# Loading the modulation's weights in blocks of 512 columns and writing four one-column products in a row

## The chip, the core and the metric

The kernel runs on one core of a Trainium2 chip. The time is the device time of one execution in microseconds (us), the median of the runs given. In the profile the engines are PE (TensorE's products) and PEld (its weight loads), DVE (VectorE), ACT (ScalarE), POOL (GpSimd) and SP (SyncE, which here only issues DMAs; SPq is its queue).

## What is computed

One decoder layer on a sequence of 1024 rows of 1024 values. The change touches one product of it, the first line here: the conditioning vector `c`, through SiLU, times a matrix of 1024 x 6144. The six parts of 1024 values shift, scale and gate the layer's two halves.

```
mod = silu(c) @ w_ada[l] + b_ada[l]
sh1, sc1, g1, sh2, sc2, g2 = [m[:, None, :] for m in jnp.split(mod, N_ADA, axis=-1)]
h = rmsnorm(x, norm1_gain[l]) * (1.0 + sc1) + sh1
proj = h @ w_in[l]
...   # stick-breaking, sliding-window and forgetting attention, a diagonal SSM, each on its columns of proj
x = x + g1 * (mixed @ w_out[l])
h = rmsnorm(x, norm2_gain[l]) * (1.0 + sc2) + sh2
x = x + g2 * (jnp.square(jax.nn.relu(h @ w_mlp_in[l])) @ w_mlp_out[l])
return rmsnorm(x, final_gain)
```

## The kernel before

The parts sh1 and sc1 are wanted at once and are made in `shift_scale` (its products are L217). The other four (indices 2 to 5: g1, sh2, sc2, g2) are made by the generator `ada_rest`, and that is what changes. It is called twice, for the parts (2, 4) and (3, 5). A call has one PSUM bank `ps` of 128 x 512: rows 0, 32, 64 and 96 each take one half (512 columns) of one of the two parts. For each of 8 slices `k` of the contraction and each of the two parts it loads the slice's 128 x 1024 weights (L303, 512 KB, tile `wa`, tag `U`, two buffers) and makes two products (L307). Each has a stationary operand of one column (`cact[:, k:k+1]`), 512 moving columns, and its own output row, so its own group of 32 columns of TensorE's array. After the eighth slice DVE adds the bias (`row`, L311) and SP stores the parts (L312).

The generator's steps are handed out by `beside(ada, 3)`, three to each of the 16 units of stick-breaking attention in `by_pair`. A unit is two `sb_row`: scores `z` (L639, with the mask's product L653), softmax on ACT and DVE, and in `mix` transposes `tp` (L700) and products with the values `pv` (L705). The products with the input weights follow in the program (`fm_unit`, `tm_unit`: L253, L254, L255 in `mm3`, three to a slice), and then the SSM (`ssm_main`: L857, L884, L886, L906), whose tiles share the tags `U` and `s4` with `ada_rest`.

What stands where on an engine is not the program's order: the tile framework's scheduler reorders all instructions by its own estimate of the times when it builds the kernel (`schedule_with_timeline_sim=True`), within the dependences. Engines and SP's queue then work strictly in the built order. Products of different kinds are so mixed on PE: attention, projections and the modulation stand between each other. Below, a visit is a run of modulation products (L307) between products of other kinds; a place where the kind changes is a change.

Of the kernel before, what the change touches and what calls it, by code (L numbers as in the profile page):

```python
# [9 lines left out]
F32 = mybir.dt.float32  # L10
# [9 lines left out]
P = 128  # L20
S = 1024
D = 1024
KT = D // P
# [10 lines left out]
def tile_trunk(ctx: ExitStack, tc: tile.TileContext, a: dict, out: bass.AP):  # L34
    nc = tc.nc
    V, A, G, T, SY = nc.vector, nc.scalar, nc.gpsimd, nc.tensor, nc.sync
# [6 lines left out]
    QD = [dram.tile([P, 3, S], F32, name=f"qd{i}") for i in range(6)]  # L43
    KD = [dram.tile([P, 2, S], F32, name=f"kd{i}") for i in range(5)]
# [28 lines left out]
    cact = const.tile([P, KT], F32, name="cact")  # L73
# [35 lines left out]
    NZ, TP, S4, NW, NWT = 2, 2, 8, 4, 2  # L109
# [80 lines left out]
    def turn(pst, tag, xs, f):  # L190
        ps = pst.tile([P, 4, P], F32, tag=tag, bufs=NZ if tag == "z" else 2, name="ps")
        for t in range(4):
            T.transpose(ps[:, t, :], xs[t][:, f * P:(f + 1) * P], ident)
        return ps.rearrange("p t k -> p (t k)")
# [95 lines left out]
                extra(t, ps)  # L290

    SPARE = lambda b: (ps1 if b else psm).tile([P, 512], F32, tag="tp" if b else "ss", bufs=TP if b else 1, name="ps")
    def ada_rest(js, wide, tile, row):

        ps = psm.tile([P, 512], F32, tag="ss", name="ps")
        for r in range(4):
            c0 = js[r // 2] * D + r % 2 * 512
            SY.dma_start(out=row[32 * r:32 * r + 1, :], in_=a["b_ada"][:, c0:c0 + 512])
        for k in range(KT):
            for i, j in enumerate(js):  # L300
                for c in range(0, D, wide):
                    w = tile()
                    SY.dma_start(out=w, in_=a["w_ada"][0, k * P:(k + 1) * P, j * D + c:j * D + c + wide])  # L303
                    yield
                    for n in range(wide // 512):
                        r = 2 * i + c // 512 + n
                        T.matmul(ps[32 * r:32 * r + 1, :], cact[:, k:k + 1], w[:, n * 512:(n + 1) * 512],  # L307
                                 start=k == 0, stop=k == KT - 1)
        for r in range(4):
            o = row[32 * r:32 * r + 1, :]  # L310
            V.tensor_tensor(o, ps[32 * r:32 * r + 1, :], o, op=ALU.add)  # L311
            SY.dma_start(out=MD[js[r // 2]][:, r % 2 * 512:r % 2 * 512 + 512], in_=o)  # L312

    def rest(x):
        for _ in x:
            pass

    v_sb = keep.tile([P, NT, 256], F32, name="v_sb")
# [273 lines left out]
    ssm = tc.alloc_tile_pool(name="ssm", bufs=1)  # L592
# [3 lines left out]
    def load_k(kd):  # L596

        kk = [[None, None], [None, None]]
        for n in (1, 0):
            for x in range(2):  # L600
                kk[x][n] = hd.tile([P, 512], F32R, tag="kk", bufs=KB, name="kk")
                SY.dma_start(out=kk[x][n].bitcast(F32), in_=kd[x * HD:x * HD + HD, :, n * 512:n * 512 + 512])
        return kk

    def load_q(qd, h, c0, c1):

        s = []
        for r in range(2):
            s.append(att.tile([P, c1 - c0], F32R, tag=f"s{r}", bufs=QB, name=f"s{r}"))
            load = SY.dma_start(out=s[r].bitcast(F32), in_=qd[h * HD:h * HD + HD, r:r + 2, c0:c1])  # L610
        return s, load.ins

    def by_pair(row, qd, kd, v, beside):

        nonlocal mark
        for p in range(2):
            kk = load_k(kd[p])
            for j in (3, 2, 1, 0):
                q = [load_q(qd[p], x, j * 256, j * 256 + 256) for x in range(2)]
                if (p, j) == MARK:  # L620
                    mark = q[1][1]
                cols_of = [slice(p * P + x * HD, p * P + x * HD + HD) for x in range(2)]
                pv, r = None, None
                for i in (2 * j, 2 * j + 1):
                    beside(8 * p + 6 - 2 * j + i % 2)
                    ws = []
                    for x in range(2):
                        w, r = row(q[x][0], kk[x], i, r, 2 * p + x)
                        ws.append([(w[:, b * P:(b + 1) * P], b) for b in range(i + 1)])
                    pv = mix(ws, v, cols_of, i, pv, r is not None)  # L630
                put(v[:, 2 * j:2 * j + 2, p * P:p * P + P], pv, r)
# [60 lines left out]
    def mix(ws, v, hs, i, pv, both):  # L692

        pv = pv or ps1.tile([P, 2, P], F32, tag="pv", bufs=1, name="pv")
        todo = [(x, ws[x][n], n) for n in range(len(ws[0])) for x in range(2)]
        for c in range(0, len(todo), 4):
            part = todo[c:c + 4]
            tp = ps1.tile([P, 4, P], F32, tag="tp", bufs=TP, name="tp")
            for b, (x, (w, kb), n) in enumerate(part):
                T.transpose(tp[:, b, :], w, ident)  # L700
            wt = att.tile([P, 4, P], F32, tag="wt", bufs=NWT, name="wt")
            copies[0] += 1
            (A.copy if copies[0] % 2 and both else V.tensor_copy)(wt[:, 0:len(part)], tp[:, 0:len(part)])  # L703
            for b, (x, (w, kb), n) in enumerate(part):
                T.matmul(pv[x * HD:x * HD + HD, i % 2, :], v[:, kb, hs[x]], wt[:, b, :],  # L705
                         start=n == 0, stop=n == len(ws[0]) - 1)
        return pv

    def put(o, pv, r):

        if r is None:
            V.tensor_copy(o, pv)
            return
        rw = att.tile([P, 2, 2, HD], F32, tag="rw", bufs=2, name="rw")
        V.tensor_copy(rw, r[:, :, :, None].to_broadcast([P, 2, 2, HD]))
        ps = ps1.tile([P, 2, P], F32, tag="tp", bufs=TP, name="ps")
        for t in range(2):
            T.matmul(ps[:, t, :], rw[:, t].rearrange("p x d -> p (x d)"), ident, start=True, stop=True)
        rb = att.tile([P, 2, P], F32, tag="rw", bufs=2, name="rb")
        A.copy(rb, ps)  # L720
        V.tensor_tensor(o, pv, rb, op=ALU.mult)
# [194 lines left out]
    def beside(x, n):  # L916
        def f(u):
            for _ in range(n):
                next(x, None)
        return f  # L920

    def ada_all():
        for js in ((2, 4), (3, 5)):
            yield from ada_rest(js, D, lambda: ssm.tile([P, D], F32, tag="U", bufs=2, name="wa"),
                                ssm.tile([P, 512], F32, tag="s4", bufs=S4, name="row"))

    ada = ada_all()
    by_pair(sb_row, QD[0:2], KD[0:2], v_sb, beside(ada, 3))
    rest(ada)
    for j, t in ((4, h2s), (3, h2b)):  # L930
        SY.dma_start(out=t, in_=MD[j].rearrange("o (k p) -> p (o k)", p=P))
# [37 lines left out]
    def out_weights(g):  # L969

        h = op.tile([P, 2, D], F32R, tag="wo", bufs=4, name="woh")
        l = op.tile([P, 2, D], F32R, tag="wo", bufs=4, name="wol")
        for b in range(2):
            raw = op.tile([P, D], F32, tag="raw", bufs=1, name="raw")
            SY.dma_start(out=raw, in_=a["w_out"][0, g * 256 + b * P:g * 256 + b * P + P, :])
            V.tensor_tensor(raw, raw, g1bc, op=ALU.mult)
            A.copy(h[:, b], raw)
            V.tensor_tensor(l[:, b], raw, h[:, b], op=ALU.subtract)
        return h, l
# [71 lines left out]
    w = None  # L1051
# [28 lines left out]
    def bank(kind):  # L1080
        n = used[kind] % 4
        used[kind] += 1
        pool, tag, bufs = ((ps2, "h", 3) if n < 3 else (psm, "ss", 1)) if kind == "x" else (
            (ps2, "t", 2) if n < 2 else (psm, "mm", 2))
        return pool.tile([P, 512], F32, tag=tag, bufs=bufs, name=kind)
# [65 lines left out]
    ws = {3: out_weights(3), 1: out_weights(1)}  # L1151
# [16 lines left out]
    def copy_of(ps):  # L1168
        t = ma.tile([P, 512], F32, tag="e", bufs=EB, name="e")
        A.copy(t, ps)  # L1170
        return t

    banks = []
    for _ in range(FIRST):
# [3 lines left out]
        r = copy_of(x)  # L1178
# [12 lines left out]
    for k, (u, b) in enumerate(zip(us, bs)):  # L1191
        ps = turn(psm, "mm", xn, k)
# [59 lines left out]
    chunks, i = [], 0  # L1252
# [24 lines left out]
    for i in range(NP):  # L1277
        if i < FIRST:
            x, r, y, pe = banks[i]
# [69 lines left out]
    def last_parts():  # L1349

        h, w = [], []
        for kind in range(4):
            gate(NP - 1, kind)
            h.append(split(rg, "a", hid[NP - 1, kind], RC2))
            w.append(split(sc, "c", raw2[NP - 1, kind], RC2))
        return h, w
# [51 lines left out]
    for c in chunks[:-1]:  # L1408
# [5 lines left out]
        for n in range(7):  # L1414
            parts = [next_both() for _ in c]
            for t in range(4):
# [4 lines left out]
                ps = xs[t] if n in on_x else ys[t]  # L1421
# [4 lines left out]
    ha, wa = last_parts()  # L1426
    for t in range(NT):
        for n in range(2):
            ps = bank("x" if n else "y")
# [61 lines left out]
```

## Time and profile before

| | |
|---|---|
| median of 3 runs | 1287.41 us (1279.86 to 1288.27) |
| the profiled execution | 1287.4 us, its span 1285.7 us |
| PE busy | 1214.4 us, 94% of the span |
| DVE, ACT, POOL busy | 955.2, 561.5, 124.9 us |
| DMA | 205.38 MB, mean 160 GB/s |
| modulation's other parts (L307) | 128 records, 209.0 to 344.0 us |
| mean granted TensorE clock | 0.979 of full speed |

A row of the timeline or of the grouped lines gives an instruction's start, its duration, engine, line, operation, tiles written and read, and shape. A product in plain float32 leaves two records of the moving operand, each with a weight load; a product in the rounded type leaves one. Products overlap: a record is longer than the time after which the next starts, so what a product takes up is read from start to start.

### The profile page before, as it was taken

What the parts mean: (1) busy time and instruction counts of PE and PEld (TensorE: products, weight loads), DVE (VectorE), ACT (ScalarE), POOL (GpSimd) and SP (SyncE); (2) the same over time, 40 slices, a digit from 0 to 9 for tenths busy, and PEclk for the clock granted to TensorE, in tenths of its full rate; (3) what the DMA queues carried; (4) which work ended last, traced back from release to release, by engine and by line L of the source; (5) the groups of instructions that cost most, each with busy time, mean ns of one, the idle gap of its engine ahead of it and who ended that gap; (6) DMA issues with size and microseconds to landing.
All of it is one profiled execution on the core that took longest, in us unless ns stands there. A gap on an engine that the chain in (4) does not pass through costs nothing.

```text
span 1285.7 us, 18756 instructions
## 1 busy us (share of the span) xinstructions
PE 1214.4 (94%) x6461; PEld 945.5 (74%) x6461; DVE 955.2 (74%) x2100; ACT 561.5 (44%) x1205; POOL 124.9 (10%) x171
## 2 busy tenths in 40 slices
PE   5899899999999988999989999999989999999994
PEld 3578677656677666878768888888867888888883
DVE  4695967775566685688998677667666777788998
ACT  4432565763233576334563333333344543433424
POOL 1219000000020100000000000000031210100003
PEclk9999899999999997899989999999999999999997
DMA  8774467567644863012124544443578653643413
GB/s 286 212 219 128 138 187 251 161 200 220 191 156 152 282 179 138 17 49 91 66 66 164 172 155 139 156 148 131 167 252 311 214 170 106 182 129 91 140 42 131
DMA packets 139336, 205.38 MB, mean 160 GB/s; under 512 B 37058, under 2 KB 77913, under 8 KB 139241
## 3 DMA queue, kind: packets, MB, share of 16 engines
q1 hardware_dynamic: 129768, 170.62, 41.4%
q0 software_dynamic: 9472, 33.56, 8.3%
q8 instruction: 51, 0.84, 0.3%
q14 instruction: 45, 0.36, 0.1%
HBM read 144.59 MB, written 59.55 MB: 159 GB/s over the span
## 4 chain that ended last, share of the span: by engine, by line
PE 78%; DVE 9%; DMA 6%; issue 2%; SPq 2%; ACT 1%; POOL 0%; DVEq 0%; POOLq 0%; ACTq 0%
PE x L255 8%; PE x L254 8%; PE x L253 8%; PE ps L253 7%; PE ps L255 6%; PE y L253 6%; PE y L254 6%; PE y L255 6%; PE ps L254 6%; PE pv L705 3%; PE tp L700 3%; PE ps L307 2%; PE z L639 2%; DMA hid<-hh 1%; DVE acc L1390 1%
## 5 line engine op out<-in xcount | busy, mean ns | idle before, releaser
L1091 ACT CAST hi<-s 128x512 fp32r<-128x512 f32 x124 | 76.0, 619 | 112.2 <-PE x L254 39.0
L1091 ACT CAST hi<-hid 128x512 fp32r<-128x512 f32 x101 | 62.2, 618 | 130.3 <-issue 58.1
L254 PE MATMUL x<-lo,hi 128*128 128x512 f32 x256 | 98.3, 390 | 0.3 <-DVE lo L1092 0.3
L253 PE MATMUL x<-hi 128*128 128x512 f32 x256 | 96.0, 390 | 2.4 <-ACT hi L1091 2.4
L255 PE MATMUL x<-hi,lo 128*128 128x512 f32 x256 | 97.8, 389 | 0.0
L1092 DVE TENSOR_TENSOR lo<-raw,hi 128x512 fp32r<-128x512 f32 x97 | 65.7, 684 | 41.3 <-PE x L255 21.7
L255 PE MATMUL ps<-hT_hi,wl 128*128 128x512 f32 x224 | 91.4, 410 | 3.0 <-DVE wl L185 3.0
L253 PE MATMUL ps<-hT_hi,wh 128*128 128x512 f32 x224 | 89.7, 412 | 4.2 <-DVE e L273 2.5
L254 PE MATMUL ps<-hT_lo,wh 128*128 128x512 f32 x224 | 90.9, 407 | 0.0
L1091 ACT CAST hi<-raw 128x512 fp32r<-128x512 f32 x97 | 59.1, 619 | 72.0 <-PE y L254 46.1
L1092 DVE TENSOR_TENSOR lo<-s,hi 128x512 fp32r<-128x512 f32 x124 | 84.0, 683 | 3.7 <-ACT hi L1091 2.6
L1092 DVE TENSOR_TENSOR lo<-hid,hi 128x512 fp32r<-128x512 f32 x101 | 68.9, 683 | 21.8 <-ACT hi L1091 19.7
L255 PE MATMUL y<-hi,lo 128*128 128x512 f32 x196 | 75.3, 389 | 0.0
L254 PE MATMUL y<-lo,hi 128*128 128x512 f32 x196 | 75.2, 389 | 0.0
L253 PE MATMUL y<-hi 128*128 128x512 f32 x196 | 73.7, 390 | 0.9 <-ACT hi L1091 0.9
L700 PE MATMUL tp<-ident,w 128*128 128x128 f32 x348 | 59.3, 289 | 3.7 <-ACT w L666 3.7
L703 DVE COPY wt<-tp 128x512 f32<-128x512 f32 (+1 forms) x68 | 42.8, 638 | 26.8 <-PE tp L700 25.2
L1273 POOL DMA_DIRECT2D raw<-in_w_mlp_out_dram x64 | 34.3, 538 | 259.5 <-DVE lo L1092 75.2
L1099 POOL DMA_DIRECT2D raw<-in_w_mlp_in_dram x16 | 14.3, 896 | 463.9 <-DVE lo L1092 390.9
L1029 DVE SCALAR_TENSOR_TENSOR x<-ps,gnr,x 128x512 f32<-128x512 f32 x64 | 46.7, 746 | 15.3 <-PE ps L255 14.8
L253 PEld LDWEIGHTS x<-hi 128*128 128x128 f32 x256 | 48.0, 188 | 13.2 <-ACT hi L1091 3.2
L639 PE MATMUL z<-kk,s 128*128 128x256 f32 (+2 forms) x192 | 54.8, 381 | 1.5 <-DMA kk<-kd 1.5
(416 smaller groups left out, 3252.7 us busy)
## 6 DMA issues: line engine op xcount, KB each, us to landing
hid<-hh SPq DMA_DIRECT2D x101, 256.0 KB
wa<-in_w_ada_dram SPq DMA_DIRECT2D x32, 512.0 KB
raw<-in_w_mlp_in_dram POOLq DMA_DIRECT2D x16, 1024.0 KB, 7.1
raw<-in_w_mlp_out_dram POOLq DMA_DIRECT2D x64, 256.0 KB, 4.3
hh<-x SPq DMA_DIRECT2D x60, 256.0 KB
hh<-h SPq DMA_DIRECT2D x49, 256.0 KB
s<-qd SPq DMA_DIRECT2D x96, 128.0 KB
wa<-in_w_ada_dram SPq DMA_DIRECT2D x32, 256.0 KB
```

Source lines behind the costliest of these rows:

```text
L253: T.matmul(ps, wh, xh, start=first, skip_group_check=more, stop=False)
L254: T.matmul(ps, wh, xl, start=False, skip_group_check=more, stop=False)
L255: T.matmul(ps, wl, xh, start=False, skip_group_check=more, stop=last)
L307: T.matmul(ps[32 * r:32 * r + 1, :], cact[:, k:k + 1], w[:, n * 512:(n + 1) * 512], start=k == 0, stop=k == KT - 1)
L639: T.matmul(z[:, 0:n], q[r][:, qs], kk[:, 0:n], start=r == 0, stop=stop and r == 1)
L700: T.transpose(tp[:, b, :], w, ident)
L703: (A.copy if copies[0] % 2 and both else V.tensor_copy)(wt[:, 0:len(part)], tp[:, 0:len(part)])
L705: T.matmul(pv[x * HD:x * HD + HD, i % 2, :], v[:, kb, hs[x]], wt[:, b, :], start=n == 0, stop=n == len(ws[0]) - 1)
L1029: V.scalar_tensor_tensor(out=x, in0=ps, scalar=r[:, t:t + 1], in1=x, op0=ALU.mult, op1=ALU.add)
L1091: A.copy(shape(hi), src)
L1092: V.tensor_tensor(shape(lo), src, shape(hi), op=ALU.subtract)
L1273: load = G.dma_start(out=raw2[i, kind], in_=w2[(2 * i + x) * P:(2 * i + x + 1) * P, n * 512:n * 512 + 512])
```

## The change

The weights come in blocks of 128 x 512 (256 KB) instead of 128 x 1024. A step of the generator loads one block; after four blocks of a slice (two halves of two parts) the program writes their four products one behind the other. The blocks use the tag `s4` with eight buffers, of which `row` holds one and, where the two calls overlap, two. `beside` hands out four steps to a unit instead of three. Bytes, products, sums and stores are the same. A blank line moves the lines behind `ada_rest` by one: L303, L307, L639, L653, L700 and L705 become L305, L308, L640, L654, L701 and L706.

```diff
-    def ada_rest(js, wide, tile, row):
+    def ada_rest(js, tile, row):
...
         for k in range(KT):
-            for i, j in enumerate(js):
-                for c in range(0, D, wide):
-                    w = tile()
-                    SY.dma_start(out=w, in_=a["w_ada"][0, k * P:(k + 1) * P, j * D + c:j * D + c + wide])
-                    yield
-                    for n in range(wide // 512):
-                        r = 2 * i + c // 512 + n
-                        T.matmul(ps[32 * r:32 * r + 1, :], cact[:, k:k + 1], w[:, n * 512:(n + 1) * 512],
-                                 start=k == 0, stop=k == KT - 1)
+            ws = []
+            for r in range(4):
+                c0 = js[r // 2] * D + r % 2 * 512
+                ws.append(tile())
+                SY.dma_start(out=ws[r], in_=a["w_ada"][0, k * P:(k + 1) * P, c0:c0 + 512])
+                yield
+            for r in range(4):
+                T.matmul(ps[32 * r:32 * r + 1, :], cact[:, k:k + 1], ws[r],
+                         start=k == 0, stop=k == KT - 1)
...
-            yield from ada_rest(js, D, lambda: ssm.tile([P, D], F32, tag="U", bufs=2, name="wa"),
+            yield from ada_rest(js, lambda: ssm.tile([P, 512], F32, tag="s4", bufs=S4, name="wa"),
...
-    by_pair(sb_row, QD[0:2], KD[0:2], v_sb, beside(ada, 3))
+    by_pair(sb_row, QD[0:2], KD[0:2], v_sb, beside(ada, 4))
```

What the scheduler makes of it shows in the built order. On PE the two kernels are the same up to the place of the first modulation product (1009 products) and again over the last 2943 of 5716. At the first place, before:

```order
L639 MATMUL z<-kk,s_2353 128x256
L639 MATMUL z<-kk,s_2355 128x256
L653 LDWEIGHTS identb
L653 MATMUL z<-mask_sb,identb 128x128
L307 MATMUL ps<-wa,cact 1x512 x2
L253 MATMUL ps<-wh,hT_hi 128x260
L254 MATMUL ps<-wl,hT_hi 128x260
L255 MATMUL ps<-wh,hT_lo 128x260
```

and after (`s` is a query tile, `kk` the keys, `wh` and `wl` the two parts of an input weight):

```order
L654 MATMUL z<-mask_sb,identb 128x128
L308 MATMUL ps<-wa,cact 1x512
L640 MATMUL z<-kk,s_2337 128x256
L640 MATMUL z<-kk,s_2339 128x256
L654 LDWEIGHTS identb
L654 MATMUL z<-mask_sb,identb 128x128
L308 MATMUL ps<-wa,cact 1x512
L253 MATMUL ps<-wh,hT_hi 128x260
```

The pair has become two single products with a score between them. Later, in the second call, where before the pairs stand like this on PE:

```order
L705 MATMUL pv<-wt,v_sb 64x128
L307 MATMUL ps<-wa,cact 1x512 x2
L705 MATMUL pv<-wt,v_sb 64x128 x5
L700 MATMUL tp<-ident,w 128x128 x3
L307 MATMUL ps<-wa,cact 1x512 x2
L700 MATMUL tp<-ident,w 128x128 x5
```

there is, after, one of the few places with four in a row, and a three:

```order
L253 MATMUL ps<-wh,hT_hi 128x260
L308 MATMUL ps<-wa,cact 1x512 x4
L706 MATMUL pv<-wt,v_sb 64x128 x6
L701 MATMUL tp<-ident,w 128x128 x8
L308 MATMUL ps<-wa,cact 1x512 x3
L640 MATMUL z<-kk,s_2693 128x256
```

Over the whole order the 64 products stand in 32 visits before, all of two. After, they stand in 49: 41 of one product, 3 of two, 3 of three, 2 of four. Without the visits, the rest of PE's order changes between `tp`, `pv` and other products in 283 stretches before and 276 after.

On SP's queue the loads of the weights stand among the loads for attention and projections. In the middle of the first call, before:

```order
L895 DMA wg<-in_w_glu_dram 128x2x256
L303 DMA wa<-in_w_ada_dram 128x1024 x3
L610 DMA s_3003<-qd_62 128x1x256
L303 DMA wa<-in_w_ada_dram 128x1024
L610 DMA s_3005<-qd_62 128x1x256
L303 DMA wa<-in_w_ada_dram 128x1024
L610 DMA s_3007<-qd_62 128x1x256
```

and after:

```order
L896 DMA wg<-in_w_glu_dram 128x2x256
L305 DMA wa<-in_w_ada_dram 128x512 x9
L611 DMA s_3031<-qd_62 128x1x256
L305 DMA wa<-in_w_ada_dram 128x512 x3
L611 DMA s_3033<-qd_62 128x1x256
L305 DMA wa<-in_w_ada_dram 128x512 x4
L611 DMA s_3035<-qd_62 128x1x256
```

There are twice as many loads of half the size in front of the same query loads.

## Rows read from the trace of the kernel before

**Rows 1.** The page: busy time and share of the span by engine.
```profile
PE 1214.4 (94%) x6461; PEld 945.5 (74%) x6461; DVE 955.2 (74%) x2100; ACT 561.5 (44%) x1205; POOL 124.9 (10%) x171
```

**Rows 2.** Windows: stretch, length, engines' busy us (records), PE clock, DMA share, GB/s.
```profile
209.00:344.00 135.00, 135.00 (x840) 83.99 (x840) 85.36 (x191) 68.83 (x155) 0.00 (x0) 1.00 0.67 208
344.00:583.00 239.00, 224.06 (x1456) 174.70 (x1453) 169.71 (x529) 113.07 (x292) 14.83 (x12) 0.95 0.44 139
583.00:1285.70 702.70, 673.83 (x2960) 547.77 (x2958) 548.12 (x967) 282.71 (x554) 58.47 (x86) 0.99 0.45 147
```

**Rows 3.** Line L307: PE's records (ns min/median/max), first and last start, waits for data.
```profile
L307 PE MATMUL ps<-wa,cact x128: 590/591/592, 209.0 to 344.0; 128*1 128x512 f32 x128
...
  DMA wa<-in_w_ada_dram: 0.2, 1
```

**Rows 4.** Timeline of PE around the first visit: start, duration, merged records.
```profile
208.04 0.28 PE L254 MATMUL ps<-wl,hT_hi 128*128 128x260 f32 x1
208.16 0.28 PE L255 MATMUL ps<-wh,hT_lo 128*128 128x260 f32 x1
...
208.52 0.23 PE L653 MATMUL z<-mask_sb,identb 128*128 128x128 bf16 x1
208.56 0.48 PE L639 MATMUL z<-kk,s 128*128 128x256 f32 x2
208.89 0.23 PE L653 MATMUL z<-mask_sb,identb 128*128 128x128 bf16 x1
209.05 1.03 PE L307 MATMUL ps<-wa,cact 128*1 128x512 f32 x4
210.00 0.39 PE L253 MATMUL ps<-wh,hT_hi 128*128 128x260 f32 x1
210.23 0.28 PE L254 MATMUL ps<-wl,hT_hi 128*128 128x260 f32 x1
```

**Rows 5.** Timeline of PE, that visit's first and last records.
```profile
209.05 0.60 PE L307 MATMUL ps<-wa,cact 128*1 128x512 f32 x2
...
209.47 0.60 PE L307 MATMUL ps<-wa,cact 128*1 128x512 f32 x2
```

**Rows 6.** Timeline of PE: products of 32 columns in `shift_scale`, four and eight.
```profile
24.45 0.43 PE L217 MATMUL ps<-wa,cact 128*32 128x128 f32 x8
...
25.06 0.64 PE L217 MATMUL ps<-wa,cact 128*32 128x128 f32 x16
```

**Rows 7.** Timeline of PE: a visit inside a run of `pv`.
```profile
251.90 0.43 PE L705 MATMUL pv<-wt,v_sb 128*64 128x128 f32 x2
252.26 1.03 PE L307 MATMUL ps<-wa,cact 128*1 128x512 f32 x4
253.22 0.44 PE L705 MATMUL pv<-wt,v_sb 128*64 128x128 f32 x4
```

**Rows 8.** Timeline of PE: a visit followed by another product of 32 columns.
```profile
266.48 1.03 PE L307 MATMUL ps<-wa,cact 128*1 128x512 f32 x4
267.34 0.38 PE L802 MATMUL ps<-tri,fpre 128*32 128x128 f32 x2
```

**Rows 9.** What SP's queue waited for, 195 to 345 us: total us, times, longest.
```profile
SPq L303 <- PE ps L307: 36.2, 17, 4.8
SPq L303 <- DMA wa<-in_w_ada_dram: 5.9, 5, 3.8
```

**Rows 10.** Line L303: the issue's duration (ns min/median/max).
```profile
L303 SPq DMA_DIRECT2D wa<-in_w_ada_dram x32: 327/334/606, 202.7 to 335.1; - x32
```

**Rows 11.** Timeline of PE: products ahead of which it stood idle, after 344 us.
```profile
408.37 0.50 PE L639 MATMUL z<-kk,s 128*128 128x512 f32 x1 [1.46 <-DMA kk<-kd]
...
428.92 0.49 PE L886 MATMUL ps<-mid 64*128 64x128 f32 x2 [0.92 <-DMA mid<-wd]
...
470.09 0.67 PE L906 MATMUL ps<-yt,wg 128*128 128x512 f32 x1 [1.74 <-DMA yt<-yd]
...
491.28 0.55 PE L733 MATMUL z<-kk,s 128*128 128x256 f32 x1 [5.12 <-DMA kk<-kd]
...
554.22 0.47 PE L253 MATMUL ps<-woh,mh 128*128 128x512 f32 x1 [1.97 <-DVE x L1029]
```

**Rows 12.** Windows of 10 us, columns as in rows 2.
```profile
480.00:490.00 10.00, 5.63 (x40) 3.75 (x38) 6.28 (x26) 8.61 (x26) 0.00 (x0) 1.00 0.99 335
490.00:500.00 10.00, 8.72 (x43) 6.02 (x44) 5.50 (x21) 3.50 (x10) 0.00 (x0) 0.66 0.34 117
500.00:510.00 10.00, 9.79 (x77) 8.38 (x76) 7.65 (x38) 8.95 (x29) 0.00 (x0) 0.87 0.15 48
510.00:520.00 10.00, 10.00 (x42) 8.66 (x42) 6.50 (x28) 5.14 (x19) 0.00 (x0) 0.50 0.08 26
520.00:530.00 10.00, 10.00 (x67) 7.62 (x65) 5.79 (x22) 3.44 (x10) 0.00 (x0) 0.94 0.01 2
```

**Rows 13.** Grouped lines: PE's records of L307, busy us, mean ns, idle before.
```profile
L307 PE MATMUL ps<-wa,cact 128*1 128x512 f32 x128 | 32.8, 591 | 0.0
```

## The prediction

> **What bounds the kernel now.** I read the page first: PE is busy for 94% of the span [rows 1], and the question is whether it is the bound where the change sits. The windows answer it: over 209 to 344 us, the stretch in which the modulation's other parts are made, PE is busy for all of its 135.00 us at full clock, while DVE has 85 and ACT 69 [rows 2]. DMA works at 0.67 of its time, and PE waited only 0.2 us for weight blocks in all [rows 3]. So in this stretch a microsecond more or less on PE is a microsecond of the stage, and loads count only if they come late. Behind it, up to 583 us, PE stands idle for 239.00 − 224.06 = 14.9 us [rows 2]: that is the only slack in which PE time could vanish, because from about 583 us on the built order of PE is the same in both kernels.
>
> **What a visit costs.** Next I read single visits in PE's timeline. At the first one, four records (two products) start at 209.05 and the next product starts at 210.00 [rows 4]. The four records come as two at 209.05 and two at 209.47 [rows 5]: both products start together and need 0.42 us for each of their two records, 0.85 us for the pair, which is what one of them needs alone. So the two run abreast, and the second is free. The 0.95 us from start to start has another 0.10 in it, and there is more at the edges: the product before the visit held PE for 0.16 us where the same one earlier held it for 0.04 (208.52 to 208.56), and the first product after it for 0.23, where its like takes 0.12 (208.04 to 208.16) [rows 4]. So a visit set into a stream of full-width products costs 0.95 + 0.12 + 0.11 = 1.18 us; one set where the kind changes anyway costs as little as 0.95 or 0.96. I take 1.07, the middle.
>
> Would four abreast cost the same as two? Rows of this trace say so for a similar shape: four products of 32 columns (8 records) last 0.43 us, eight of them 0.64 [rows 6]. A second four thus adds 0.21 us, and 0.21 is a quarter of 0.85, what one product of 128 moving columns needs alone. Four abreast cost as much as one. It follows that the cost goes by visits, not by products: one product alone costs as much as four.
>
> Does a single overlap a neighbour of another kind? The visit at 252.26 is the eleventh, of the first part, in columns 0 to 63 of the array; the `pv` behind it is the second head's, in columns 64 to 127. It still starts only 0.96 us later [rows 7]. Where a product of the visit's own width follows, it starts after 0.86 us [rows 8]. So an overlap with another width isn't seen, and the change of width costs about 0.1.
>
> The Trainium skill, in "TensorEngine Tiling (Array Packing)", section Key Properties, has a rule for this: a change of the tiling mode, and not merely of the tile, drains the engine. The trace agrees (0.96 against 0.86). Without such a drain the 17 visits below would cost 17 × 0.86 = 14.6 us; with the rows' price they cost 18.2. The rule speaks against this change as built, since single products mean more changes of mode.
>
> **The change part by part.** *Visits.* The diff reads as if 32 visits of two became 16 of four. The built order shows otherwise: the scheduler places each product by itself, and there are 49 visits, 41 of them of one product. That is 17 more: 17 × 1.07 = **+18.2 us** on PE, between 17 × 0.96 = 16.3 and 17 × 1.18 = 20.1.
>
> *The rest of PE's order.* It has 276 stretches of a kind where it had 283. A change costs 0.1 to 0.2 us (0.11 and 0.12 above), so 7 fewer give **−1.0 us** (−0.7 to −1.4).
>
> *Loads.* The bytes stay 16.8 MB; there are 64 issues instead of 32, 32 × 0.334 = 10.7 us more of SP's time [rows 10]. SP has it: in this stretch it stood for 36.2 us in front of weight loads, waiting for a visit to free a buffer [rows 9]. Queued behind those are the query loads of attention and the input weights, and PE's scores wait for them. Before, a load had two buffers; now six or seven blocks are on their way (1.5 to 1.8 MB against 1.0), so a product can come later after its load's issue. For it speaks the 0.2 us of waits in 32 visits; 49 at that rate give **+0.3 us**. The other end is the 5.9 us for which SP itself waited for earlier blocks to land [rows 9], if all of that became PE's. I take the low value because PE's own waits are the nearest row.
>
> *Buffers.* The SSM's tiles also use `s4`, so its early loads (`vtd`, `ed`) now stand behind nearly all the weight blocks. Their first reader, L857, comes after the last visit in both orders, so this costs nothing; if it came late, it would add to the wait on `mid` [rows 11], 0.9 us. DVE's eight additions and the stores are unchanged, and the second half's scale is read far behind 583 us.
>
> *What the idle time behind takes back.* The visits hold back everything on PE. But chains that run on other engines and DMA go on meanwhile, and waits on these shrink. From 0 to 14.9 us can vanish so. I split it by its rows [rows 11]: the waits for keys at 408 (1.46), for the SSM's `mid` at 429 (0.92) and for `yt` at 470 (1.74) end with such chains, which start from loads and ACT or DVE work in the stages before; together **−4.1 us**. The 5.12 us at 491 wait for a load of keys in a burst of loads (DMA 0.99 busy at 480 to 490 [rows 12]) that is released by PE's own progress, and the 1.97 us at 554 wait for DVE reading PE's banks: both move along with PE, and I leave them.
>
> Sum: 18.2 − 1.0 + 0.3 − 4.1 = **+13.4 us** on the profiled execution's 1287.4 us, which equals the median of the runs shown (1287.41). Forecast **1301 us**, with its own range of 1295 to 1307 from the ends of the visits' and the waits' prices. About 1%, 12.9 us, is what a measurement of this kernel can tell from no change; the forecast lies just at it, 1300.3 us.
>
> **The rivals.** *Taken back behind* (not slower). The idle 14.9 us after 344 vanish entirely, since PE comes later to every wait: 1287.4 + 18.2 − 1.0 + 0.3 − 14.9 = 1290 us. For it: most of these waits end with a DMA. Against it: DMAs are issued in SP's order behind PE's buffers. It decides if the waits at 491 and 554 fall too. With them could go the clock's dip: behind the gap at 480 to 490, in which PE was busy for 5.63 us of 10, the granted clock falls to its lower level for parts of the next 40 us, 1.2 for 2.4 GHz [rows 12]. The shares 0.66, 0.87, 0.50, 0.94 lose 3.4 + 1.3 + 5.0 + 0.6 = 10.3 us. If that is saved too, the time is 1280 us.
>
> *Blocks come late* (slower still). Work between first and last visit is shorter in the new order (368 other products instead of 610), so the same 16.8 MB must come in less time, with 0.67 of DMA taken already. In the built order a product waits for its own block. If PE takes over the 5.9 us, and the gap drops the clock as at 510 to 520 (5.0 us), the time is 1301 + 10.9 = 1312 us.
>
> *Four abreast after all* (faster). If the products ran as the program writes them, 16 visits fewer would give 1287.4 − 16 × 1.07 = 1270 us. It takes an engine that overlaps singles with other kinds; rows 7 show none. The Trainium skill's "TensorEngine Tiling (Array Packing)", section Theoretical Speedup, allows up to four times for operands of 32 columns or fewer, which rows 6 bear out for products that stand together; only two visits of four do.
>
> **How the numbers follow.** Forecast 0.50 (0.36 of it above 1300.3, 0.14 below), taken back 0.33 (0.05 of it with the clock), late blocks 0.13, four abreast 0.04. Slower by over 1%: 0.36 + 0.13 = 0.49; within: 0.14 + 0.33 = 0.47; faster: 0.04. The range leaves out the four abreast, the clock's case and a part of the late blocks: **1286 to 1313**.
>
> **What would show it.** In the new profile the start of L308 should still be at 209 us, and its records should take up 49 × 1.03 = 50 us of PE's time instead of 32.8 [rows 13]. PE should stay fully busy up to the last of them, and its total busy time should rise from 1214 by some 17 us. The last 703 us should be unchanged. The forecast is wrong if PE waits for `wa` by more than 1 us in all (late blocks), if the gaps behind the stage fall under 5 us or the clock keeps its full level through them (taken back), or if a product of another kind starts less than 0.9 us after a single one (abreast).

## The result and the profile after

The changed kernel takes **1304.62 us** (median of 6 runs, 1300.2 to 1306.8), the kernel before 1286.2 us in 6 runs; the ratio is 1.0145, with a 95% interval of 1.0115 to 1.0176. It is slower by 18 us. The profiled execution took 1304.78 us, 17.4 more than that of before.

The page's first part, busy time by engine, answers to [rows 1]: PE is busier by 17.4 us, the others nearly as before.

```profile
PE 1231.8 (95%) x6461; PEld 948.6 (73%) x6461; DVE 956.1 (73%) x2100; ACT 561.7 (43%) x1205; POOL 125.3 (10%) x171
```

The windows cut at the same three places of PE's order as [rows 2]: first to last visit, from there to where the two orders meet again, and the rest.

```profile
211.02:314.67 103.65, 103.65 (x570) 48.99 (x569) 62.42 (x125) 51.74 (x115) 0.00 (x0) 1.00 0.67 214
314.67:601.14 286.47, 270.66 (x1727) 210.67 (x1725) 193.24 (x593) 129.67 (x330) 14.76 (x12) 0.96 0.43 136
601.14:1303.00 701.86, 674.06 (x2962) 548.30 (x2961) 549.24 (x971) 283.48 (x557) 58.59 (x86) 0.99 0.45 147
```

The visits' stretch is shorter because less other work stands in it, and still PE is busy for all of it. From the first visit to the meeting point it is 390.1 us, before 373.6: 16.5 us more. The 2.0 us by which the first visit starts later (211.02 against 209.05) lie in an order that is the same in both (the trace's clock record has two stretches of 3.4 us at the lower level there that before lacks), and the last stretch gives 1.2 back.

The line of the products, by its trace and by the grouped lines, answers to [rows 3, 13]. The 128 records are as long as before (591 ns), but together they take up 50.0 us instead of 32.8, since fewer of them lie beside each other.

```profile
L308 PE MATMUL ps<-wa,cact x128: 590/591/592, 211.0 to 314.7; 128*1 128x512 f32 x128
...
  DMA wa<-in_w_ada_dram: 0.7, 3
```

```profile
L308 PE MATMUL ps<-wa,cact 128*1 128x512 f32 x128 | 50.0, 591 | 0.0
```

Two places of PE's timeline say it directly (answering to [rows 4, 6]). In the first a visit holds one product (2 records), in the second four (8 records).

```profile
282.70 1.02 PE L308 MATMUL ps<-wa,cact 128*1 128x512 f32 x2
283.64 0.33 PE L706 MATMUL pv<-wt,v_sb 128*64 128x128 f32 x2
```

```profile
276.73 1.04 PE L308 MATMUL ps<-wa,cact 128*1 128x512 f32 x8
277.70 0.33 PE L706 MATMUL pv<-wt,v_sb 128*64 128x128 f32 x2
```

To the next product it is 0.94 us behind one, 0.97 behind four. There are 49 visits, as the order said, and SP's queue still stands mostly in front of weight loads until a visit frees a buffer, as in [rows 9]:

```profile
SPq L305 <- PE ps L308: 39.9, 32, 3.4
```

Behind the stage PE's idle time is 286.47 − 270.66 = 15.8 us, 14.9 before. The waits of [rows 11] have gone, become smaller or moved (the second and the third row here are of the same lines as those for `yt` and at 491 us there), and others have come:

```profile
465.70 0.44 PE L640 MATMUL z<-kk,s 128*128 128x384 f32 x1 [2.31 <-DVE m L680]
...
496.66 0.70 PE L907 MATMUL ps<-yt,wg 128*128 128x512 f32 x1 [1.15 <-ACT sgm L909]
...
515.64 0.55 PE L734 MATMUL z<-kk,s 128*128 128x256 f32 x1 [3.54 <-issue]
...
575.24 0.34 PE L1011 MATMUL ps<-ones,sq 128*128 128x1 f32 x1 [4.25 <-DVE gnv L86]
```

### The profile page after: what moved, and what is told of

It reads as the page before. It is cut to its first block, busy times and chain, and to the rows that moved or that the text cites. A ratio compares the mean times of both kernels' runs of the same rounds, so it can differ in the third digit from the quotient of the medians.

```text
span 1303.0 us, 18811 instructions
## 1 busy us (share of the span) xinstructions
PE 1231.8 (95%) x6461; PEld 948.6 (73%) x6461; DVE 956.1 (73%) x2100; ACT 561.7 (43%) x1205; POOL 125.3 (10%) x171
## 4 chain that ended last, share of the span: by engine, by line
PE 82%; DVE 8%; DMA 5%; ACT 2%; issue 2%; SPq 1%; DVEq 0%; ACTq 0%
PE x L255 8%; PE x L254 8%; PE x L253 8%; PE ps L253 7%; PE ps L254 7%; PE ps L255 6%; PE y L255 6%; PE y L253 6%; PE y L254 6%; PE ps L308 4%; PE pv L706 4%; PE tp L701 3%; PE z L640 3%; DMA raw<-in_w_out_dram 1%; DMA hid<-hh 1%
## 5 line engine op out<-in xcount | busy, mean ns | idle before, releaser
L253 PE MATMUL x<-hi 128*128 128x512 f32 x256 | 95.9, 390 | 2.4 <-ACT hi L1092 2.4
L253 PE MATMUL ps<-hT_hi,wh 128*128 128x512 f32 x224 | 90.7, 417 | 4.8 <-DVE e L273 2.6
L253 PE MATMUL y<-hi 128*128 128x512 f32 x196 | 73.6, 390 | 0.6 <-ACT hi L1092 0.6
L701 PE MATMUL tp<-ident,w 128*128 128x128 f32 x348 | 59.4, 288 | 7.1 <-ACT w L667 5.5
L640 PE MATMUL z<-kk,s 128*128 128x256 f32 (+2 forms) x192 | 56.3, 387 | 2.9 <-DVE m L680 2.9
L701 PEld LDWEIGHTS tp<-ident,w 128*128 128x128 f32 x348 | 39.5, 143 | 25.2 <-issue 13.6
L253 PEld LDWEIGHTS x<-hi 128*128 128x128 f32 x256 | 48.0, 188 | 13.2 <-ACT hi L1092 3.2
```

Of the source, the lines that this page charges most:

```text
L253: T.matmul(ps, wh, xh, start=first, skip_group_check=more, stop=False)
L640: T.matmul(z[:, 0:n], q[r][:, qs], kk[:, 0:n], start=r == 0, stop=stop and r == 1)
```

## The experiments

Theory: a visit of up to four products has a price on PE, nearly whatever it holds, PE is the bound, and so the time goes by the number of visits. Rivals: the loads (twice as many, half as large, in other buffers) and the other order of everything behind; or that PE's time is taken back by idle time behind the stage.

The table at the end of this section has all runs side by side.

**Four in a row, with the change's loads.** The first product of a slice now is the one that needs the slice's last block, and the others are queued behind it:

```diff
-            for r in range(4):
-                T.matmul(ps[32 * r:32 * r + 1, :], cact[:, k:k + 1], ws[r],
-                         start=k == 0, stop=k == KT - 1)
+            first = None
+            for r in (3, 0, 1, 2):
+                with tc.issue_after(first) if first else nullcontext():
+                    mm = T.matmul(ps[32 * r:32 * r + 1, :], cact[:, k:k + 1], ws[r],
+                                  start=k == 0, stop=k == KT - 1)
+                first = first or mm.ins
```

> The loads in blocks of 512 columns and their buffers stay; the four products of a slice wait for the slice's last block, so they stand in a row: 16 visits of four on PE, against 49 in the changed kernel and 32 before. Theory of visits (a visit costs about 1.07 us however many of the four products are in it): 33 visits fewer than the changed kernel, 33 x 1.07 = 35 us, 1304.6 - 35 = 1269 us; against the kernel before 16 fewer, 17 us, a ratio of 0.987. Rival, the loads: twice as many, half as large, more of SP's queue, and another order of everything behind cost the 18 us; then it stays near 1304. Rival, four of 512 columns don't run abreast: a visit takes 1.9 us, 16 of them as long as 32 of 0.96, and the time is that of before, 1286.

Measured 1268.3 us, ratio to before 0.9845 (0.9812 to 0.9879). The grouped lines show what the products take up, and the windows the stretch from first visit to meeting point:

```profile
L310 PE MATMUL ps<-wa,cact 128*1 128x512 f32 x128 | 16.6, 591 | 2.7 <-DMA wa<-in_w_ada_dram 2.7
```

```profile
213.20:560.80 347.60, 337.06 (x2271) 255.75 (x2271) 248.35 (x706) 179.57 (x438) 14.71 (x12) 0.97 0.56 173
```

The same 128 records take up 16.6 us, a third of 50.0: four of 512 columns do run abreast, in the 0.97 us from start to start that the visit of four took above. The rival of the loads falls, since all of the change's loads are still there, and so does the one that four take twice as long. This kernel beats both others. It now pays a little for loads: PE waited 2.7 us for blocks.

**Pairs, with the change's loads.** The same edit with the pairs (1, 0) and (3, 2) instead of all four.

```diff
-            for r in range(4):
-                T.matmul(...)
+            for q in (0, 2):
+                first = None
+                for r in (q + 1, q):
+                    ...   # as above
```

> The loads in blocks of 512 columns and their buffers stay; the products stand in pairs as before, each pair waiting for its second block: 30 visits. Theory of visits: two fewer than before, 1286 - 2 = 1284 us, within 0.5% of before. Rival, the loads, their issues and the other order they bring: 1300 us or more, as in the changed kernel.

Measured 1275.4 us, 0.9894 (0.9862 to 0.9927): faster than before by more than the theory of visits said, and far from the rival's 1300.

```profile
210.10:568.60 358.50, 349.86 (x2292) 255.84 (x2291) 251.98 (x717) 180.30 (x444) 14.66 (x12) 0.99 0.54 170
```

PE stood idle for 358.50 − 349.86 = 8.6 us here against 14.9 before. By the trace's record of the clock it was busy at the lower of its two levels (1.2 instead of 2.4 GHz) for 7.4 us of this stretch, before for 23.0. Below, PE's work is its busy time in the whole execution less half of the part of it at the lower level, and the clock's loss is that half. The work here is 1205.1 − 11.1 = 1194.1 us, before 1214.4 − 19.2 = 1195.2: two visits fewer, 1.1 us. So the theory's term was right; the rest of the gain came from waits and clock. The profiled execution is the fastest of the six (1271.1 us, at a granted clock of 0.984; the others have 0.976 to 0.979), so a part of that gain belongs to this one execution.

**Each product twice, in the kernel before.**

```diff
-                        T.matmul(ps[...], cact[:, k:k + 1], w[...], start=k == 0, stop=k == KT - 1)
+                        for again in range(2):
+                            T.matmul(ps[...], cact[:, k:k + 1], w[...],
+                                     start=k == 0 and again == 0, stop=k == KT - 1 and again == 1)
```

> The kernel before with each of the 64 products of the modulation's other parts made twice, the second added to the first (so these parts are twice the product): a visit lasts 0.85 us longer, 30 visits with 64 added products, 32 x 0.85 = 27 us more of PE's time in the stage, and nothing else that is new to load. If all of it reaches the end: 1286 + 27 = 1313 us. If the waits behind the stage take 4 us of it, as the prediction had it: 1309. If they take all their 15 us: 1298.

Measured 1309.1 us, 1.0164 (1.0126 to 1.0201). PE's work rose by 27.2 us, but the time only by 20 (1309.1 against 1289.0, measured beside it): in the stretch, idle time and the clock's loss fell by 4.0 and 4.7 us.

```profile
210.20:602.80 392.60, 381.67 (x2420) 261.78 (x2419) 253.21 (x718) 182.90 (x445) 14.91 (x12) 0.98 0.50 156
```

**Few products, in the kernel before.**

```diff
-                        T.matmul(ps[...], cact[:, k:k + 1], w[...], start=k == 0, stop=k == KT - 1)
+                        if k in (0, KT - 1):
+                            T.matmul(ps[...], cact[:, k:k + 1], w[...], start=k == 0, stop=k == KT - 1)
```

> The kernel before with all its loads, but of the eight slices of the contraction only the first and the last are multiplied for the four other parts (the six between are left out): 7 visits instead of 32. If a visit's 1.07 us reaches the end both ways: 25 fewer, 1286 - 27 = 1259 us. If with less on PE another limit of the stage (softmax on ACT and DVE, loads) shows at once, less than half of that is gained: above 1272.

Measured 1269.08 us, 0.9838 (0.98 to 0.9877): 20 us, between the two cases. PE's work fell by 28.7 us, near the theory's 27, but idle time rose by 5.1 and the clock's loss by 4.8.

```profile
213.20:569.20 356.00, 336.03 (x2195) 259.83 (x2195) 250.82 (x717) 181.09 (x444) 14.70 (x12) 0.95 0.55 172
```

**Four in a row, with the loads of before.** One part of the change without the other: blocks of 128 x 1024 in two buffers.

```diff
         for k in range(KT):
+            ws = []
+            for j in js:
+                ws.append(tile())
+                SY.dma_start(out=ws[-1], in_=a["w_ada"][0, k * P:(k + 1) * P, j * D:j * D + D])
+                yield
+            ...   # four products in a row, as above, from ws[r // 2]
```

> The kernel before's loads (128 x 1024, two buffers of tag U) with the four products of a slice in a row, waiting for the slice's second load: 16 visits without the change's blocks. Theory of visits: 16 fewer than before, 17 us by 1.07 each (the run with blocks and 16 visits had 22 us less of PE's work): 1265 to 1272 us, and at most 3 us of waits for weights. Rival, the blocks matter: with two buffers no load runs ahead of a visit, PE waits for weights at each of the 16 visits by 1 us or more, and the gain is gone: 1280 us or more.

Measured 1268.65 us, 0.9868 (0.9836 to 0.99): as with the small blocks.

```profile
212.20:561.80 349.60, 334.59 (x2271) 252.62 (x2271) 254.23 (x712) 179.23 (x441) 15.93 (x12) 0.98 0.55 174
```

Neither the blocks nor their buffers matter here. What the change wrote down, four products behind each other, brought 17 to 21 us in these two orders when they really stood so, with either kind of load.

**More visits.** The changed kernel with `beside(ada, 8)` instead of `beside(ada, 4)`: the built order has 57 visits.

> The changed kernel with eight steps of the generator to a unit instead of four, which gives another built order: 57 visits instead of 49. Theory of visits, at the 1.02 us that the changed kernel's PE work showed: 8 more, 8 us more of PE's work between the first visit and the place where the orders meet; 1304.6 + 8 = 1313 us, plus or minus what the waits behind the stage do (they moved by -13 to +10 us between the runs so far). Rival, the 18 us belong to the loads and not to the visits: PE's work stays as in the changed kernel, within 2 us.

Measured 1303.31 us, 1.0136 (1.0101 to 1.0171), not slower than the changed kernel. PE's work rose by 10.0 us, more than the 8 expected, and the loads' rival falls. But idle time fell by 8.2 us and the clock's loss by 5.5, so the visits' price did not reach the time here.

```profile
210.80:596.80 386.00, 378.39 (x2295) 254.84 (x2293) 250.92 (x714) 181.37 (x444) 14.74 (x12) 0.99 0.51 158
```

**Four in a row in another order.** The first experiment with `beside(ada, 8)`.

> The run with four products in a row, with eight steps to a unit instead of four: 16 visits again, in another built order. Theory of visits: PE's work between the first visit and the meeting point within 2 us of that run's 325 us. What the waits and the clock behind the stage do differs by the order alone: 1260 to 1278 us. If waits behind the stage are set by how early PE is done, they stay as in that run, and the time is within 3 us of 1268.

Measured 1282.7 us, 0.9966 (0.9943 to 0.9989), 14 us slower than the first experiment with the same 16 visits and the same PE work (1177.9 and 1177.8 us), and 4.7 us outside the range expected. Idle time in the stretch is 21.1 us instead of 10.5, the clock's loss the same (11.8 and 11.9). So of the first experiment's gain of 21 us this order keeps 3. The largest piece is one wait. In PE's and DVE's timelines:

```profile
490.70 0.58 PE L722 MATMUL ps<-ident,rw 128*128 128x128 f32 x1 [8.09 <-DVE rw L719]
```

```profile
489.22 1.23 DVE L980 TENSOR_TENSOR raw<-raw,g1bc 128x1024 f32<-128x1024 f32 x1 [8.53 <-DMA raw<-in_w_out_dram]
490.36 0.29 DVE L719 COPY rw<-r 128x256 f32<-128x256 f32 x1
```

and in the windows the clock behind it (0.52):

```profile
490.00:500.00 10.00, 9.16 (x41) 7.86 (x42) 8.55 (x33) 5.94 (x18) 0.00 (x0) 0.52 0.43 115
```

DVE stood 8.5 us in its queue in front of a block of the output weights that had been asked for only at 478.59 us and took 10.6 us to land; the copy that PE needed stood behind it, though it had nothing to do with those weights. In the chain of work it is one piece:

```profile
478.59 10.61 DMA raw<-in_w_out_dram
```

**The output weights off DVE.** The same kernel with the two DVE lines of `out_weights` on GpSimd.

```diff
-            V.tensor_tensor(raw, raw, g1bc, op=ALU.mult)
+            G.tensor_tensor(raw, raw, g1bc, op=ALU.mult)
             A.copy(h[:, b], raw)
-            V.tensor_tensor(l[:, b], raw, h[:, b], op=ALU.subtract)
+            G.tensor_tensor(l[:, b], raw, h[:, b], op=ALU.subtract)
```

> The run with four in a row and eight steps to a unit, in which PE stood idle for 8.09 us at 490 us because DVE waited 8.53 us in its queue for a block of the output weights (the line that multiplies it by the gate) with the softmax's work queued behind. Here that line and the subtraction two lines on go to GpSimd, so DVE no longer stands in front of that load. If that wait made the difference between the two runs with 16 visits (1282.7 and 1268.3 us): about 8 us less idle and the clock's dip behind it (half of it 5 us) gone, 1268 to 1274 us. If the waits only move to another place: 1279 to 1285 us.

Measured 1278.5 us, 0.9934 (0.9906 to 0.9961), next to the 1279 to 1285 expected if the waits only move; the interval overlaps that of the run without it. That wait shrank to 1.9 us, but elsewhere a new one came, on a norm made by DVE; PE's waits by total time (times, longest):

```profile
PE ps L1014 <- DVE gnr L92: 7.1, 1, 7.1
PE ps L722 <- DVE rw L719: 1.9, 1, 1.9
```

So that block explains where the 8 us lay in that run, but taking it away is not worth 8 us.

**The same in the first experiment.**

> The same two lines moved to GpSimd in the run with four in a row and four steps to a unit (1268.3 us), where no wait on the output weights over 1.6 us stood on PE. If such waits are what is left to gain, at most 7 us idle and the dip's 12 us: 1255 to 1268 us. If GpSimd, slower and with its own loads behind, holds up the output projection, 1270 us or more.

Measured 1272.64 us, 0.9886 (0.9854 to 0.9918): nothing gained against 1268.3. Its profiled execution, 8 us above the median, has a wait of 3.5 us at the output projection (L253).

All runs. Work is that of the whole profiled execution; idle time and the clock's loss are those of its stretch from the first visit to the meeting point. The work behind the meeting point, where the order is the same in all, comes out between 669.9 and 672.3 us, so the work is known to about 2 us. The runs come from four sets of measurements, each with the kernel before beside it, and compare by the ratio. Idle time and the clock's loss are of one execution each. The kernel before, in one order, took 1280.4 us with a granted clock of 0.981 and 1295.1 us with 0.972.

| run | visits | median us | ratio | profiled us | work | idle | clock's loss |
|---|---|---|---|---|---|---|---|
| before | 32 | 1286.2 | 1 | 1287.4 | 1195.2 | 14.9 | 11.5 |
| changed | 49 | 1304.6 | 1.0145 | 1304.8 | 1213.9 | 15.8 | 7.5 |
| four in a row | 16 | 1268.3 | 0.9845 | 1265.8 | 1177.8 | 10.5 | 11.9 |
| pairs | 30 | 1275.4 | 0.9894 | 1271.1 | 1194.1 | 8.6 | 3.7 |
| products twice | 30 | 1309.1 | 1.0164 | 1310.4 | 1222.4 | 10.9 | 6.8 |
| few products | 7 | 1269.1 | 0.9838 | 1272.5 | 1166.5 | 20.0 | 16.3 |
| four, loads of before | 16 | 1268.7 | 0.9868 | 1266.3 | 1179.1 | 15.0 | 6.2 |
| more visits | 57 | 1303.3 | 1.0136 | 1303.2 | 1223.9 | 7.6 | 2.0 |
| four, other order | 16 | 1282.7 | 0.9966 | 1282.9 | 1177.9 | 21.1 | 11.8 |
| same, weights on GpSimd | 16 | 1278.5 | 0.9934 | 1280.4 | 1178.9 | 19.8 | 10.7 |
| four in a row, weights on GpSimd | 16 | 1272.6 | 0.9886 | 1280.9 | 1175.4 | 17.6 | 15.2 |

The expectations' 325 us of work and 1.02 us a visit were taken from the stretch alone, with PE counted as busy for all of the time at the lower level. That doesn't compare well: PE stood idle for a part of that time (5.5 of 20.5 us in the changed kernel), and in the kernels with 16 visits the first visit stands some 20 records later in PE's order, so the stretch holds less other work.

## Why the prediction was right, and where not

**The visits**, the term that carried the sum, were right in mechanism and nearly in size. The order's 49 visits against 32 were there in the profile, the records took up 50.0 us for a predicted 50, and PE's work rose by 1213.9 − 1195.2 = 18.7 us; the prediction's three terms for it (18.2 − 1.0 + 0.3) make 17.5. Over all runs with the same 64 products the work goes by visits: 1177.8 us at 16 (the mean of five runs, 1175.4 to 1179.1), 1194.1 at 30, 1195.2 at 32, 1213.9 at 49, 1223.9 at 57. From 16 to 32 that is 1.09 us a visit, from there to 49 1.10, over all 41 visits 1.12. The prediction's 1.07 stands a little below, inside its own bounds of 0.96 and 1.18.

**Loads and buffers** were rightly left near nothing: PE's products and weight loads waited 0.7 us for blocks where 0.3 had been counted, and with 16 visits both kinds of load give the same time. The rival of late blocks did not come about. DMA's share in the stage was 0.67, as before.

**What the idle time behind takes back** is the step that failed. It was put at −4.1 us, because three waits would shrink. The waits on `mid` and on keys at 408 did go, and in front of the products that had waited for `yt` and at 491 PE waited 1.15 and 3.54 us, but others came (2.31 and 4.25 us among the rows above): idle time behind the first visit rose by 0.9 us. Argued from single waits of the old order, this couldn't be seen, because behind the first visit there is no old order any more: each built order has its own waits. That is shown by the two kernels with 16 visits and equal PE work whose idle time differs by 10.6 us, and whose times by 14. With this term at +0.9 in place of −4.1 the sum would have been 18.4, 1305.8 us.

Over the whole profiled execution the span grew by 17.3 us: 18.7 of work, −1.3 of the clock's loss, −0.1 of idle time. The prediction had no term for the clock. That it added so little is luck: it lost 4.0 us less in the stretch and 2.7 more outside, where the work is the same.

**The rival that PE's time is taken back behind** did not happen in this change, but it has something to it. In the run with 57 visits 10.0 us more of PE's work than in the changed kernel were taken back whole, and of the 27.2 us of the doubled products 9 were. Idle time and the clock's loss together are 9.6 us at 57 visits, 23.3 at 49, 26.4 at 32, 21.2 to 32.9 at 16 and 36.3 at 7, so in the main less where PE has more to do; but the pairs, with two visits fewer than before, have 12.3, and five kernels with 16 visits spread over 12 us. Whether there is a rule in it, or only the chance of the orders and of single executions, stays open; a kernel with a fixed order behind the stage, which would tell, wasn't tried.

**Four abreast** was rightly given little chance for the kernel as built, since the scheduler issues each product when its own block is in. It was right about the chip, though: forced into a row, four cost what one does. That the predicted 1270 us came as 1268.3 is partly the order's luck: with the same visits another order took 1282.7.

## What to carry to other kernels

Products on separate column groups overlapped here only where they stood in a row in the built order; where a scheduler places each by its own data, make the first of them wait for the last data and queue the others behind it, and count the visits in the built order instead of trusting the loop. In a stage where PE never idles, count what an edit adds to PE's work start to start, by visits and not by records. That is the price on PE; what of it reaches the time is less sure. Where the order behind the edit changes as well, allow some 10 us each way for waits and clock, and don't book single waits of the old order as gains.

## What was not expected of the hardware

A visit of four plain float32 products with one column each takes 0.97 us to the next product, one alone 0.94 to 0.95: the three others cost 0.02 to 0.03 us in all. It ends at four: six products (12 records), as stood in one visit in the run with 57, take 1.81 us.

```profile
276.53 1.88 PE L308 MATMUL ps<-wa,cact 128*1 128x512 f32 x12
278.34 0.33 PE L706 MATMUL pv<-wt,v_sb 128*64 128x128 f32 x2
```

Short gaps on PE can cost nearly as much again in clock. In the changed kernel's windows around the waits of 3.54 and 4.25 us (at 515 and 575 us):

```profile
510.00:520.00 10.00, 5.93 (x38) 4.92 (x38) 5.03 (x25) 6.14 (x26) 0.00 (x0) 0.63 0.65 226
520.00:530.00 10.00, 10.00 (x66) 8.07 (x66) 7.89 (x39) 4.38 (x14) 0.00 (x0) 0.86 0.07 22
...
570.00:580.00 10.00, 4.96 (x22) 4.43 (x21) 10.00 (x25) 3.20 (x5) 0.00 (x0) 0.70 0.14 41
580.00:590.00 10.00, 10.00 (x36) 7.98 (x36) 6.80 (x16) 2.36 (x7) 0.00 (x0) 0.78 0.11 38
```

Each gap has 10.2 us at the lower level behind its start (from 512.6 and from 574.1 us, by the clock's record). PE was busy for 6.7 and 8.3 us of them, so the clock cost 3.3 and 4.1 us on top of the 4.1 and 5.0 us for which PE stood idle in these windows.
